# Two more pairs of split buffers ahead of the last gate: the tiles that brought m back are kept for it

## The chip, the cores and the metric

The kernel runs on one core of a Trainium2 chip. Five engines work beside each other: TensorE (PE in the profile, its weight loads PEld) multiplies, VectorE (DVE) and ScalarE (ACT) do elementwise work, GpSimd (POOL) some more of it, and SyncE (SP) issues most of the transfers. The metric is the device time of one execution in microseconds (us), lower is better. It is given as the median of several runs.

## The reference

One layer of a decoder trunk on 256 tokens of width 2048, all in float32:

```
h = rmsnorm(x);  u = h @ w_in                       # 16 half-width and 2 full-width fields
ya = b * conv3(c * xa) * silu(za)                   # branch A
yb = rmsnorm_per_head(hgrn2(q, f, iv)) * silu(og)   # branch B
m = sigmoid(ga) * (ya @ w_a) + sigmoid(gb) * (yb @ w_b)
x = x + m @ w_o
x = x + sigmoid(rmsnorm(x) @ w_pg) * (p @ w_pp)
out = rmsnorm(x)
```

The change touches the last two products, `m @ w_o` and `rmsnorm(x) @ w_pg`, both of a 256 x 2048 operand with a 2048 x 2048 weight.

## The kernel before

**Split products.** A float32 product is made from three reduced products. Each weight tile of 128 x 1024 that a load has brought (a half of a `raw` tile) is split by `cut` (lines 194 to 197): ScalarE copies it rounded into `whi`, VectorE subtracts and gets `wlo`. The operand is held split in the same way (`xh` and `xl`, or `mh` and `ml` for m), and `triple` issues hi x hi, hi x lo and lo x hi into one accumulator. So each weight tile costs one load of half a megabyte, one ScalarE and one VectorE instruction, and TensorE twelve matmuls of 512 columns (two token tiles, two slices of the contraction).

**Items and positions.** All weight tiles are laid in one list, `items`; the place in it is the position `pos` of the main loop. There are 275. Positions 213 to 244 are the four column groups of `m @ w_o` (kind O, eight tiles each, the first two interleaved). Positions 245 to 274 are the gate product (kind PG). Its first two column groups are computed together, at positions 245 to 258: for the chunks 3 and 5 of the contraction (`LATE_SEVEN`) by seven products of quarter blocks instead of eight (kind S, positions 251 and 254, 21 matmuls each), for the other six chunks plainly (kind C, two positions a chunk, 12 matmuls each). Group 2 is at 259 to 266, and the last, group 3, at 267 to 274 (`last_group`), which is run through three times, by token tile and half of the columns, so that its eight split pairs have to stay. The code calls position 245 `gate` and 254 `settled`.

**Buffers.** A split is put into a pair of buffers, which `free_pair` hands out. Four pairs lie in the pool `wp`. From position 245 on the pool `late`, opened in the place of the operand `m`, has five more; `rings` keeps per pool until which position each pair is taken, and the pool whose oldest pair comes free first gives it. Loads go to three `raw` tiles in `wp` (two positions each) and, for some chunks, to a fourth in `late`. `m` itself is written to DRAM for three of its four column groups and read back by `unpark` into tiles of the pool `back` (five tiles of 128 x 1024), transposed and split into `mT`. `back` is closed at position 229.

**How far ahead.** `ahead(pos)` says how many positions ahead of TensorE weights are split: 3, 4 from position 249, 5 from 255, growing to 8 at 265. Loads are issued four positions ahead of the splits, and wait for their `raw` tile.

**Chunks of seven products.** `combine_late` adds the quarter blocks of the raw tile of an S position on VectorE (four adds of 128 x 512), splits one quarter into a small pair `bhi` and `blo`, and at the next position splits the two rows of sums into two pairs (`free_pair`, twice). With the split that every position has, an S position takes three pairs.

**Epilogues.** They are generators that move on by one `yield` per position (`advance`; twice at an S position). `ep_o` adds a finished group of `m @ w_o` to x (line 879), squares it, writes it to DRAM and back to transpose it (`turned`: four writes, a read, after `lag` further steps the VectorE transpose of line 354), then splits it with a gain into `x1T` (lines 319 and 320). The lags are 3, 3, 6 and 7 for the four groups. `ep_products` (from line 752; the copy of line 756, the adds of line 747) puts the seven products together at position 256; it reads the PSUM banks P1, P6, P5 and P7. There are four banks of the kind "g"; group 2 of the gate takes the banks of P1 and P6 for its first and second token tile.

**What sets the order.** Instructions are emitted position by position: splits first, then matmuls, loads, epilogues. A planner orders each engine's instructions from that by its own estimate of when they are ready, TensorE's too. For ScalarE and VectorE `pinned` fixes the order of emission at positions 239 to 256 (and at 140 to 212). SP's and TensorE's queues stay the planner's. Each queue runs in order: what waits at its head holds what is behind it.

Of the kernel before, what the change touches and what calls it, by code (L numbers as in the profile page):

```python
# [9 lines left out]
F32 = mybir.dt.float32  # L10
F32R = mybir.dt.float32r
# [4 lines left out]
P = 128  # L16
# [7 lines left out]
CW = 512  # L24
# [24 lines left out]
def hybrid_kernel(ctx, tc, xT, x, pT, prm, gfin, masks, w_in, w_a, w_b, w_o, w_pg, w_pp, out):  # L49
    nc = tc.nc  # L50

    const = ctx.enter_context(tc.tile_pool(name="const", bufs=1))
    wp = ctx.enter_context(tc.tile_pool(name="wp", bufs=1))
# [6 lines left out]
    pools, closers = {}, {}  # L60

    def open_pool(name, side):
        closers[name] = ExitStack()
        pools[name] = closers[name].enter_context(
            tc.tile_pool(name=name, bufs=1, side=side, reuse_waits="tile")
        )

    def close_pool(name):
        closers.pop(name).close()
        del pools[name]  # L70
# [3 lines left out]
    state = {"tmp": "tmp1"}  # L74
# [3 lines left out]
    def nm(s):  # L78
        uid[0] += 1
        return f"{s}_{uid[0]}"  # L80

    def t4(tag="t4", bufs=None):
        bufs = bufs or {"tmp1": 8, "tmp2": 1, "tmp3": 5}[state["tmp"]]
        return pools[state["tmp"]].tile([P, 1024], F32, tag=tag, bufs=bufs, name=nm(tag))

    def bank(tag):
        return ps.tile([P, CW], F32, tag=tag, bufs=4, name=nm(tag))
# [19 lines left out]
    items = []  # L107
    for gi, (kind, j, w, g, op) in enumerate(groups):
# [3 lines left out]
        for c in range(w.shape[2]):  # L112
            it = {"gi": gi, "kind": kind, "j": j, "c": c, "last": c == w.shape[2] - 1, "op": op}
            if not units:
                key = ("PP", j // 2) if kind == "PP" else (gi, c // 2)
# [13 lines left out]
    def raw_of(pos):  # L129
        it = items[pos]  # L130
        if it["raw"] not in loaded:
            if it["kind"] == "S" and it["op"] == "hT":
                t = tuple(
                    pools["st"].tile([P, n, CW], F32, tag=tag, bufs=bufs, name=nm(tag))
                    for tag, n, bufs in (("sA", 2, 2), ("sB", 1, 3))
                )
            else:
                n = it["c"] if it["j"] == 0 else 4 + 4 * (it["j"] - 1) + it["c"] // 2
                spare = it["op"] == "x1T" and n and n % 4 == 0
                pool, bufs = (pools["late"], 1) if spare else (wp, 3)  # L140
                t = pool.tile([P, 2, 2 * CW], F32, tag="raw", bufs=bufs, name=nm("raw"))
            loaded[it["raw"]] = t
        return loaded[it["raw"]]
# [39 lines left out]
    def pair_of(pool, n, tags=("whi", "wlo"), width=2 * CW):  # L183
        return tuple(pool.tile([P, width], F32R, tag=tag, bufs=n, name=nm(tag)) for tag in tags)

    rings = {"wp": 4 * [-1], "late": 5 * [-1]}

    def free_pair(until):
        names = [n for n in rings if n == "wp" or n in pools]
        name = min(names, key=lambda n: rings[n][0])  # L190
        rings[name] = rings[name][1:] + [until if until < last_group else len(items)]
        return pair_of(pools.get(name, wp), len(rings[name]))

    def cut(hi, lo, src):
        a = nc.scalar.activation(out=hi, in_=src, func=AF.Copy)  # L195
        v = nc.vector.tensor_tensor(out=lo, in0=src, in1=hi.bitcast(F32), op=ALU.subtract)  # L196
        state["splits"] = (a.ins, v.ins)
# [15 lines left out]
    def combine_late(pos):  # L213
        R = raw_of(pos)
        (b11, b21), (b12, b22) = ([R[:, n, i * CW : (i + 1) * CW] for i in range(2)] for n in range(2))
        add(b11, b11, b12)
        add(b12, b12, b22)
        ts = [pair_of(pools["late"], 1, ("bhi", "blo"), CW)]
        cut(*ts[0], b22)
        add(b22, b11, b22)  # L220
        add(b21, b22, b21)
        yield
        for n in range(2):
            hi, lo = free_pair(pos)
            cut(hi, lo, R[:, n, :])
            ts += [(hi[:, i * CW : (i + 1) * CW], lo[:, i * CW : (i + 1) * CW]) for i in range(2)]
        b22, t1, t4_, t3, t2 = ts
        sums[pos] = (b22, t1, t3, t2, t4_)
# [15 lines left out]
    last_group = len(items) - w_pg.shape[2]  # L244
    gate = next(n for n, it in enumerate(items) if it["op"] == "x1T")
    settled = max(n for n, it in enumerate(items) if it["kind"] == "S")
# [3 lines left out]
    LEAD, AHEAD = 3, 4  # L250
    FIRST = 4
# [53 lines left out]
    def gain(base, k):  # L305
        return prm_t[:, base + k : base + k + 1]
# [28 lines left out]
    def blocks(ap):  # L335

        return ap.rearrange("p (c b e) -> p c b e", b=4, e=32)

    def spread(ap, t):

        return ap.rearrange("p (b c t e) -> p t c b e", b=4, c=4, t=NT)[:, t]

    def to_dram(src, tag, bufs, queue=nc.sync):
        d = dram.tile([P, 4, T], F32, tag=tag, bufs=bufs, name=nm(tag))
        to = d.rearrange("(b i) a x -> a i b x", b=4)
        for a in range(4):
            queue.dma_start(out=to[a], in_=src[32 * a : 32 * a + 32, :].rearrange("i (b x) -> i b x", b=4))  # L350
        return d

    def square_turn(dst, src):
        nc.vector.transpose(
            out=dst.rearrange("p (k a e) -> p a k e", a=4, e=32), in_=src.rearrange("p (a k e) -> p a k e", a=4, e=32)
        )

    def turned(src, lag, dst=None, queues=(nc.sync, nc.sync)):
        d = to_dram(src, "turn", 3, queues[0])
        yield  # L360
        queues[1].dma_start(out=src, in_=d.rearrange("p a x -> p (a x)"))
        for _ in range(lag):
            yield
        dst = t4() if dst is None else dst
        square_turn(dst, src)
        return dst
# [379 lines left out]
    def add(out, a, b):  # L746
        nc.vector.tensor_tensor(out=out, in0=a, in1=b, op=ALU.add)  # L747
# [100 lines left out]
            state["m", j] = to_dram(m, f"m{j}", 1)  # L848
            yield

    def back():
        return pools["back"].tile([P, 1024], F32, tag="back", bufs=5, name=nm("back"))

    def unpark():

# [18 lines left out]
    def ep_o(j, psum):  # L874
        xs = state["x"]
        src = t4()
        for t in range(NT):
            d = xs[:, t, j * CW : (j + 1) * CW]
            nc.vector.tensor_tensor(out=d, in0=d, in1=psum[t], op=ALU.add)
            nc.scalar.activation(  # L880
                out=src[:, t * CW : (t + 1) * CW], in_=d, func=AF.Square,
                accum_out=state["ss2"][:, t * 4 + j : t * 4 + j + 1],
            )
        x1 = src
        for t in range(NT):
            nc.scalar.activation(
                out=spread(x1, t), in_=blocks(xs[:, t, j * CW : (j + 1) * CW]), func=AF.Copy
            )
        x1 = yield from turned(x1, (3, 3, 6, 7)[j])
        for c in range(4):  # L890
            put(state["x1T"], j * 4 + c, x1[:, c * T : (c + 1) * T], gain(PRM_GPLE, j * 4 + c))
        for c in LATE_SEVEN:
            if c // 2 == j:
                yield
                yield from late_sums(c)
        if j == 3:
            tot = sc(2, "tot2", 1)
            nc.vector.tensor_reduce(
                out=tot, in_=state["ss2"].rearrange("p (t j) -> p t j", t=NT),
                axis=mybir.AxisListType.X, op=ALU.add,  # L900
            )
            state["rstd2"] = rsqrt_of(tot, NT, D, "r2")
# [212 lines left out]

    def ahead(pos):

        return LEAD + min(max(pos - gate, 0) // 4, 5 if pos > settled else 1)

    def triple(psum, op, part, first, last):  # L1120
        (oh, ol), (hi, lo) = op, part
# [7 lines left out]
    used, left = {}, {}  # L1129
# [57 lines left out]
    combining = {}  # L1187
    banks = {}
    psums = {}
    done = 0  # L1190
    for pos, it in enumerate(items[:last_group]):
        mark = len(nc.cur_bb.bb.instructions)
        kind, j, c, last = (it[n] for n in ("kind", "j", "c", "last"))
        _, _, w, g, opname = groups[it["gi"]]
        nch = w.shape[2]
        if kind == "O" and j == 2 and c == 0:
            close_pool("back")
        if pos == gate:
            close_pool("m")
            open_pool("late", "left")  # L1200
        if pos == parked:
            close_pool("st")
            open_pool("m", "left")
            state["mT"] = operand(pools["m"], "m", KT)
            open_pool("back", "left")
            active.append(unpark())
        if items[pos + 2]["kind"] == "S" and items[pos + 2]["op"] == "hT":
            combine_weights(pos + 2)
        for q in range(pos + 1, done):
            if items[q]["kind"] == "S" and items[q]["op"] != "hT" and q not in sums:  # L1210
                next(combining.setdefault(q, combine_late(q)), None)
        while done < min(pos + 1 + ahead(pos), len(items)):
            if done < 2:
                for i in range(2):
# [56 lines left out]
                for t in range(NT):  # L1271
                    product(psum[t], state[opname], k, t, hi[:, s], lo[:, s], k == 0, k == 2 * nch - 1)

        for q in range(done, min(done + AHEAD, len(items)) if pos >= FIRST else 0):
            load(q)
        if 0 <= pos - TOKENS < 4:
            load_tokens(pos - TOKENS)
# [33 lines left out]
    for t, halves in ((0, (0, 1)), (1, (0,)), (1, (1,))):  # L1311
        bk, n = bank("g"), CW // 2
# [16 lines left out]
    finish()  # L1329
    close_pool("tmp3")  # L1330
    close_pool("late")


# [70 lines left out]
```

## Time and profile before

| | |
|---|---|
| median of 3 runs | 816.7 us (816.34 to 816.7) |
| profiled execution | 815.29 us |
| its span in the profile | 813.5 us |
| TensorE busy | 802.3 us (99%) |
| VectorE busy | 607.0 us (75%) |
| ScalarE busy | 463.0 us (57%) |
| transfers | 198.52 MB, 244 GB/s on average |

Times in the profile count from the start of the span. A row of the timeline gives the start of an instruction, or of a run of like instructions (x and their number), its length, the engine, the line of the code, what it writes and reads, and in brackets how long the engine sat idle before it and what ended that. A wait for several things is put down to the one that came last. A matmul's length is a model, so a loss on TensorE is read from the distance between two starts. Windows give the busy time of each engine in a stretch of the span, with the number of instructions, the granted clock and the busy share of the DMA engines.

### The profile page before, as it was taken

To read this page: it belongs to the slowest core of one execution; us is meant where nothing else is said; L and a number is where in the kernel's file an instruction comes from. 1 tells how busy PE (TensorE), PEld (TensorE's weight loads), DVE (VectorE), ACT (ScalarE), POOL (GpSimd) and SP (SyncE) were. 2 spreads that over 40 slices of the span, in tenths; PEclk is the share of its full clock that TensorE was granted. 3 is DMA by queue.
4 is the path that set the end of the run, shared out by engine and by line. 5 is a ranking of instruction groups with operands and counts; after the bars stand their busy time and mean duration, and the time that the engine had idled before them with its cause. 6 is when DMAs were issued, how large, how long until landed. Compare 5 with 4: busy or idle time off the path is not lost.

```text
span 813.5 us, 10701 instructions
## 1 busy us (share of the span) xinstructions
PE 802.3 (99%) x4053; PEld 663.2 (82%) x4053; DVE 607.0 (75%) x780; ACT 463.0 (57%) x624; POOL 59.9 (7%) x58
## 2 busy tenths in 40 slices
PE   9999999999999999999999999999999999999995
PEld 6888888888888888888888888888888888887885
DVE  6746588767765498767679988987987656779972
ACT  7576476465555466466455556456545455665733
POOL 1000000001000000000021200210000000000280
PEclk9999999999999999999999999999999999999999
DMA  9988555648867555648799996996844779885722
GB/s 337 396 306 290 195 202 172 232 137 274 251 235 253 191 179 200 207 155 268 263 334 293 320 306 214 319 307 208 255 157 179 283 244 322 298 282 199 315 78 103
DMA packets 53812, 198.52 MB, mean 244 GB/s; under 512 B 6913, under 2 KB 16385, under 8 KB 40065
## 3 DMA queue, kind: packets, MB, share of 16 engines
q1 hardware_dynamic: 44352, 174.78, 60.7%
q0 software_dynamic: 6384, 16.25, 8.4%
q10 hardware_dynamic: 3024, 6.82, 2.5%
q8 instruction: 31, 0.51, 0.2%
q14 instruction: 21, 0.16, 0.1%
HBM read 184.19 MB, written 13.63 MB: 243 GB/s over the span
## 4 chain that ended last, share of the span: by engine, by line
PE 96%; issue 1%; ACT 1%; DMA 0%; DVE 0%; POOLq 0%; POOL 0%; ACTq 0%
PE g L1122 27%; PE g L1124 27%; PE g L1123 27%; PE s L1123 4%; PE s L1124 4%; PE s L1122 4%; PE s L530 1%; DMA praw<-in_pT 0%; ACT whi L195 0%; PE s L631 0%; PE s L650 0%; PE s L649 0%; PE s L648 0%; ACT xs L985 0%; ACT xh L319 0%
## 5 line engine op out<-in xcount | busy, mean ns | idle before, releaser
L196 DVE TENSOR_TENSOR wlo<-raw,whi 128x1024 fp32r<-128x1024 f32 (+1 forms) x266 | 319.0, 1216 | 151.4 <-ACT whi L195 149.6
L195 ACT ACTIVATE whi<-raw 128x1024 fp32r<-128x1024 f32 (+1 forms) x266 | 274.2, 1049 | 197.8 <-PE g L1124 163.9
L1122 PE MATMUL g<-whi,xh 128*128 128x512 f32 (+1 forms) x676 | 260.0, 385 | 0.0
L1124 PE MATMUL g<-whi,xl 128*128 128x512 f32 (+1 forms) x676 | 259.6, 384 | 0.0
L1123 PE MATMUL g<-wlo,xh 128*128 128x512 f32 (+1 forms) x676 | 259.6, 384 | 0.0
L1124 PEld LDWEIGHTS g<-whi,xl 128*128 128x128 f32 x676 | 127.0, 188 | 25.3
L1123 PEld LDWEIGHTS g<-wlo,xh 128*128 128x128 f32 x676 | 127.0, 188 | 25.0
L1122 PEld LDWEIGHTS g<-whi,xh 128*128 128x128 f32 x676 | 127.0, 188 | 24.8
L1123 PE MATMUL s<-wlo,xh 128*128 128x512 f32 x136 | 53.0, 390 | 0.0
L1124 PE MATMUL s<-whi,xl 128*128 128x512 f32 x136 | 53.0, 390 | 0.0
L1122 PE MATMUL s<-whi,xh 128*128 128x512 f32 x136 | 52.1, 390 | 0.2 <-ACT xh L319 0.2
L1123 PE MATMUL g<-wlo,mh 128*128 128x512 f32 x128 | 49.8, 389 | 0.0
L1124 PE MATMUL g<-whi,ml 128*128 128x512 f32 x128 | 49.7, 390 | 0.0
L1122 PE MATMUL g<-whi,mh 128*128 128x512 f32 x128 | 49.5, 389 | 0.0
L195 ACT ACTIVATE thi<-sA 128x1024 fp32r<-128x1024 f32 x15 | 15.9, 1062 | 32.4 <-DVE sA L747 20.1
L1122 PEld LDWEIGHTS s<-whi,xh 128*128 128x128 f32 x136 | 25.5, 188 | 5.8 <-ACT xh L319 0.6
L1123 PEld LDWEIGHTS s<-wlo,xh 128*128 128x128 f32 x136 | 25.5, 188 | 5.6 <-DVE wlo L196 0.3
L1124 PEld LDWEIGHTS s<-whi,xl 128*128 128x128 f32 x136 | 25.5, 188 | 5.5 <-DVE xl L320 0.2
L1124 PEld LDWEIGHTS g<-whi,ml 128*128 128x128 f32 x128 | 23.9, 188 | 5.2 <-DVE ml L830 0.3
L1122 PEld LDWEIGHTS g<-whi,mh 128*128 128x128 f32 x128 | 24.0, 188 | 5.0
L1123 PEld LDWEIGHTS g<-wlo,mh 128*128 128x128 f32 x128 | 24.0, 188 | 5.0
L1122 PE MATMUL g<-whi,yaTh 128*128 128x512 f32 x64 | 24.9, 389 | 0.0
(243 smaller groups left out, 980.8 us busy)
## 6 DMA issues: line engine op xcount, KB each, us to landing
raw<-in_w_in SPq DMA_DIRECT2D x66, 1024.0 KB, 4.9
raw<-in_w_o SPq DMA_DIRECT2D x16, 1024.0 KB, 6.3
sT<-in_w_in POOLq DMA_DIRECT2D x30, 512.0 KB, 9.6
raw<-in_w_in SPq DMA_DIRECT2D x28, 512.0 KB, 5.7
raw<-in_w_a SPq DMA_DIRECT2D x8, 1024.0 KB, 8.5
raw<-in_w_b SPq DMA_DIRECT2D x8, 1024.0 KB, 8.8
raw<-in_w_pg SPq DMA_DIRECT2D x16, 512.0 KB, 6.3
raw<-in_w_pg SPq DMA_DIRECT2D x8, 1024.0 KB, 7.2
```

The lines of the kernel that those rows point to most:

```text
L195: a = nc.scalar.activation(out=hi, in_=src, func=AF.Copy)
L196: v = nc.vector.tensor_tensor(out=lo, in0=src, in1=hi.bitcast(F32), op=ALU.subtract)
L530: nc.tensor.matmul(out, X[:, 0, h, s], X[:, 1, h, t], start=True, stop=True, tile_position=(0, i * n))
L1122: nc.tensor.matmul(psum, oh, hi, start=first, stop=False)
L1123: nc.tensor.matmul(psum, oh, lo, start=False, stop=False)
L1124: nc.tensor.matmul(psum, ol, hi, start=False, stop=last)
```

## The change

The tiles of `back` stay open to the end. At position 233 four of them are taken as two pairs of split buffers, and from there `free_pair` hands out, of all pairs in one list `held`, the one that comes free first: six pairs from 233, nine from 245 (three pairs in `late` in the place of five). `back` now lies below `m` on the stack, where `m` lay, and `late`, with three pairs and one raw tile, fills the place of `m`. The small pair `bhi`, `blo` becomes the two halves of a tile `t4` of the third part's pool.

`ahead` is 4 from position 233, 5 from 237 and 8 from 255. The loads run three positions ahead of the splits instead of four from 245 to 253. The fourth raw tile serves position 254 first instead of 252 (then 261 and 269). The second step of `combine_late` is taken two positions ahead of its S position at the earliest. The lag of the last group's transpose is 5 instead of 7.

```diff
-    def t4(tag="t4", bufs=None):
+    def t4(tag="t4", bufs=None, dtype=F32):
         bufs = bufs or {"tmp1": 8, "tmp2": 1, "tmp3": 5}[state["tmp"]]
-        return pools[state["tmp"]].tile([P, 1024], F32, tag=tag, bufs=bufs, name=nm(tag))
+        return pools[state["tmp"]].tile([P, 1024], dtype, tag=tag, bufs=bufs, name=nm(tag))
...
-                spare = it["op"] == "x1T" and n and n % 4 == 0
+                spare = it["op"] == "x1T" and n > 1 and n % 4 == 1
...
-    rings = {"wp": 4 * [-1], "late": 5 * [-1]}
+    held = []
 
     def free_pair(until):
-        names = [n for n in rings if n == "wp" or n in pools]
-        name = min(names, key=lambda n: rings[n][0])
-        rings[name] = rings[name][1:] + [until if until < last_group else len(items)]
-        return pair_of(pools.get(name, wp), len(rings[name]))
+        if "back" not in state:
+            held.append([until, pair_of(wp, 4)])
+            del held[:-4]
+            return held[-1][1]
+        it = min(held, key=lambda it: it[0])
+        assert it[0] < state["pos"]
+        it[0] = until if until < last_group else len(items)
+        return it[1]
...
-        ts = [pair_of(pools["late"], 1, ("bhi", "blo"), CW)]
+        b = t4(dtype=F32R)
+        ts = [(b[:, :CW], b[:, CW:])]
...
-    def back():
-        return pools["back"].tile([P, 1024], F32, tag="back", bufs=5, name=nm("back"))
+    def back(dtype=F32):
+        return pools["back"].tile([P, 1024], dtype, tag="back", bufs=5, name=nm("back"))
...
-        x1 = yield from turned(x1, (3, 3, 6, 7)[j])
+        x1 = yield from turned(x1, (3, 3, 6, 5)[j])
...
     def ahead(pos):
 
-        return LEAD + min(max(pos - gate, 0) // 4, 5 if pos > settled else 1)
+        if pos > settled:
+            return LEAD + 5
+        return LEAD + min(max(pos - gate + 16, 0) // 4, 2)
...
-        if kind == "O" and j == 2 and c == 0:
-            close_pool("back")
+        if pos == gate - 12:
+            state["back"] = [back(F32R) for _ in range(4)]
+            held.extend([-1, tuple(state["back"][i : i + 2])] for i in (0, 2))
         if pos == gate:
             close_pool("m")
             open_pool("late", "left")
+            held.extend([-1, pair_of(pools["late"], 3)] for _ in range(3))
         if pos == parked:
             close_pool("st")
+            open_pool("back", "left")
             open_pool("m", "left")
             state["mT"] = operand(pools["m"], "m", KT)
-            open_pool("back", "left")
             active.append(unpark())
...
             if items[q]["kind"] == "S" and items[q]["op"] != "hT" and q not in sums:
-                next(combining.setdefault(q, combine_late(q)), None)
+                if q not in combining or q <= pos + 2:
+                    next(combining.setdefault(q, combine_late(q)), None)
...
-        for q in range(done, min(done + AHEAD, len(items)) if pos >= FIRST else 0):
+        for q in range(done, min(done + AHEAD - (gate <= pos < settled), len(items)) if pos >= FIRST else 0):
             load(q)
...
     close_pool("late")
+    close_pool("back")
```

More of the change, by code (lines that the diff above doesn't have):

```diff
@@ L1191, in hybrid_kernel @@
     for pos, it in enumerate(items[:last_group]):
-        mark = len(nc.cur_bb.bb.instructions)
+        mark, state["pos"] = len(nc.cur_bb.bb.instructions), pos
         kind, j, c, last = (it[n] for n in ("kind", "j", "c", "last"))
```

## The prediction

> **What bounds the kernel now.** I read the page first, for the engine that fills the span and the chain that ended last.
>
> ```profile
> span 813.5 us, 10701 instructions
> ## 1 busy us (share of the span) xinstructions
> PE 802.3 (99%) x4053; PEld 663.2 (82%) x4053; DVE 607.0 (75%) x780; ACT 463.0 (57%) x624; POOL 59.9 (7%) x58
> ```
>
> TensorE is the bound. The change takes no matmul away, so it can win only what TensorE loses in idle time. The view of what TensorE waited for and the windows of the last stages say how much that is and where.
>
> ```profile
> PE s L1014 <- DVE warm L1010: 1.5, 1, 1.5
> PE g L1122 <- ACT whi L195: 0.7, 2, 0.4
> PE s L1122 <- ACT xh L319: 0.2, 1, 0.2
> ```
>
> ```profile
> 629.00:716.30 87.30, 87.30 (x385) 72.02 (x385) 58.52 (x65) 47.22 (x65) 0.57 (x1) 1.00 0.82 290
> 716.30:744.80 28.50, 28.50 (x126) 23.38 (x125) 24.79 (x33) 15.13 (x22) 0.00 (x0) 1.00 0.80 280
> 744.80:749.10 4.30, 3.44 (x13) 1.78 (x12) 3.50 (x9) 4.26 (x7) 0.72 (x1) 1.00 0.00 2
> 749.10:760.40 11.30, 11.30 (x51) 9.36 (x50) 11.02 (x12) 8.52 (x10) 0.00 (x0) 1.00 0.84 323
> ```
>
> The first wait is at the start of the kernel and stays. The other two fall into one window of 4.3 us. Before and after it TensorE is full: 126 matmuls in 28.50 us, 0.226 us each. TensorE's timeline there (four rows of one matmul each left out) tells the loss exactly.
>
> ```profile
> 744.82 0.39 PE L1124 MATMUL s<-whi,xl 128*128 128x512 f32 x1
> 745.40 0.50 PE L1122 MATMUL s<-whi,xh 128*128 128x512 f32 x1 [0.20 <-ACT xh L319]
> ...
> 746.72 0.39 PE L1124 MATMUL s<-whi,xl 128*128 128x512 f32 x1
> 747.55 0.50 PE L1122 MATMUL g<-whi,shi 128*128 128x512 f32 x1 [0.44 <-ACT whi L195]
> 747.88 0.40 PE L1122 MATMUL s<-whi,xh 128*128 128x512 f32 x1
> 748.50 0.73 PE L1122 MATMUL g<-whi,shi 128*128 128x512 f32 x2 [0.22 <-ACT whi L195]
> 749.07 0.39 PE L1123 MATMUL g<-wlo,shi 128*128 128x512 f32 x1
> ```
>
> From 744.82 to 749.07 are 4.25 us, in which 11 matmuls started: 4.25 - 11 x 0.227 = 1.75 us lost. TensorE first waits for the last group's `xh`, the tail of `m @ w_o`, and then for the two combined pairs of position 254. This 1.75 us, 0.21% of 816.7, is all that the change can win. VectorE's and ScalarE's timelines say who made TensorE wait.
>
> ```profile
> 719.44 1.28 DVE L879 TENSOR_TENSOR xs<-xs,g 128x512 f32<-128x512 f32 x2
> 723.66 1.23 DVE L196 TENSOR_TENSOR wlo<-raw,whi 128x1024 fp32r<-128x1024 f32 x1 [2.94 <-ACT whi L195]
> ...
> 725.74 1.22 DVE L196 TENSOR_TENSOR wlo<-raw,whi 128x1024 fp32r<-128x1024 f32 x1
> ...
> 727.47 2.35 DVE L196 TENSOR_TENSOR wlo<-raw,whi 128x1024 fp32r<-128x1024 f32 x2
> 729.86 1.42 DVE L747 TENSOR_TENSOR raw<-raw 128x512 f32<-128x512 f32 x2
> ...
> 733.25 5.76 DVE L196 TENSOR_TENSOR wlo<-raw,whi 128x1024 fp32r<-128x1024 f32 x5
> ...
> 742.43 1.22 DVE L196 TENSOR_TENSOR wlo<-raw,whi 128x1024 fp32r<-128x1024 f32 x1
> 743.57 1.24 DVE L354 STREAM_TRANSPOSE t<-t 128x1024 f32<-128x1024 f32 x1
> ```
>
> ```profile
> 744.84 1.71 ACT L319 ACTIVATE xh<-t,prm_t 128x256 fp32r<-128x256 f32 x4 [6.99 <-DVE t L354]
> 746.46 6.73 ACT L195 ACTIVATE whi<-raw 128x1024 fp32r<-128x1024 f32 x7
> 754.75 1.06 ACT L195 ACTIVATE whi<-raw 128x1024 fp32r<-128x1024 f32 x1 [1.56 <-DMA raw<-in_w_pg]
> 755.71 0.58 ACT L756 ACTIVATE t<-g 128x512 f32<-128x512 f32 x1
> ```
>
> From 723.66 VectorE works without a pause up to the transpose at 743.57; ScalarE stands 6.99 us in front of `xh`, behind that transpose. VectorE's queue in the order of emission is the limit of this stage, not the transfer of the transpose.
>
> **The change part by part.**
>
> *Split buffers and the lead.* Pairs free from position 233 let two splits more be done before the gate. After the add to x at 719.44, VectorE has ten splits ahead of the transpose now (the rows of 1, 1, 2, 5 and 1). With two positions more of lead these begin at position 250 in place of 248, and with lag 5 the transpose still stands behind the split of 255: eight splits. Two splits are 2.35 us (the row at 727.47). So the transpose comes at 743.57 - 2.35 = 741.22 and `xh` at 742.49, ahead of the 744.82 at which TensorE wants it. Its wait goes.
>
> The two splits move to 684 to 716, where in the window from 629 VectorE is busy 58.52 of 87.30 us, ScalarE 47.22. Their loads (a megabyte) go there too; DMA engines are free for 18% of those 87.3 us, 15.7 us. I cost them at nothing: TensorE has three split positions in hand, 36 matmuls, 8.2 us. If that cover went, it would cost TensorE the wait for a load. One place there is tight: group 2's transpose already waits for its DMA, and the add at 719.44 is behind it in the queue.
>
> ```profile
> 713.73 1.25 DVE L354 STREAM_TRANSPOSE t<-t 128x1024 f32<-128x1024 f32 x1 [0.33 <-DMA t<-turn]
> ```
>
> Each microsecond by which an early split holds up group 2's write would come off the 2.35. Bounds: 0, and 1.2 for one split; I take 0, since `back` is free before TensorE gives a pair back, which lets a split start earlier.
>
> *What is late next: the combined pairs of 254.* They now stand behind the split of 256. VectorE takes up its splits 3.96 us after the transpose:
>
> ```profile
> 747.53 8.04 DVE L196 TENSOR_TENSOR wlo<-raw,whi 128x1024 fp32r<-128x1024 f32 x7 [0.19 <-ACT whi L195]
> 755.84 1.23 DVE L196 TENSOR_TENSOR wlo<-raw,whi 128x1024 fp32r<-128x1024 f32 x1 [0.28 <-ACT whi L195]
> 756.98 0.68 DVE L747 TENSOR_TENSOR t<-t,g 128x512 f32<-128x512 f32 x1
> ```
>
> That is 741.22 + 3.96 = 745.18 now, and 1.15 us for each of seven: 256, the two of 254, then 257 to 260. The second of 254 is ready at 745.18 + 3 x 1.15 = 748.6, 1.2 earlier than now (749.83). TensorE can meanwhile run position 255, 12 matmuls or 2.7 us from 745.05, to 747.8, and then the first pair's six, 1.4 us, to 749.1. No wait if the planner orders it so; up to 0.5 us if it takes 254's four first matmuls as early as now. The next bound covers that.
>
> *The new queue in front of the banks.* At position 255 the lead jumps to 8: four splits (260 to 263), and 264 at 256, are emitted ahead of `ep_products`, and the order is pinned there. Before, only 261 stood between 260 and `ep_products` (the single rows at 754.75 and 755.84). Position 259, group 2, needs the banks that `ep_products` reads: its second token tile wants P6, free with the add at 756.98, while it starts only here:
>
> ```profile
> 760.42 0.39 PE L1122 MATMUL g<-whi,xh 128*128 128x512 f32 x1
> ```
>
> With 1.75 us won it starts at 758.67 and wants P6 three matmuls on, at 759.35. When is P6 free? The load of 261 waits for its raw tile, released by the second split of 254, as now:
>
> ```profile
> 749.91 22.82 SPq L160 DMA_DIRECT2D raw<-in_w_pg  x7
> DMA to landing us min/median/max: 4.7/7.2/7.9
> ```
>
> (The second line gives the landing times of all the gate's megabyte loads.) It is issued 0.08 us after that split, 748.7. From issue to ScalarE's start took 754.75 - 749.91 = 4.84 us: 753.5. VectorE follows 1.09 later (755.84 against 754.75), 754.6; four splits, 4.6; the add, 0.68: 759.9. Against 759.35 that is a delay of 0.57. Bounds by the fastest and slowest landing of the gate's megabyte loads, 4.7 and 7.9 us: delay 0.4 and 3.6. I take 4.84, the same load from the same releaser, at a time when the DMA engines stand idle (share 0.00 in the window up to 749.1). The load of 263, issued 2.3 us ahead, is the only other one.
>
> [...] No run here shows this load in its new place; the 4.84 above is the nearer row.
>
> *What costs nothing.* The `t4` tile in place of `bhi`, `blo`: the same two instructions each, and the slots it takes were last used by group 1's sums and group 2's transpose, long done; cover gone, the adds of 254 wait behind it. The exchange of `back` and `m` in memory: SP's reads of m might wait for other tiles than now, with the loads of `w_o` queued behind; bounds 0 and the stage's lead of 8.2 us, taken as 0. The new places of the raw tile and one load less of lead: 254 takes the room of `m`, free at 716.3, 19 us ahead of its split. The other queues, POOL and the scalar DMA queue, get nothing new. The last group is split at the pace of freed pairs as now, and TensorE does not wait there.
>
> Sum: -1.75 + 0.57 = -1.18, and 0.08 for handing over, as from split to load above: -1.1 us. The profiled execution is 815.29, which gives 814.2; the median is 1.4 above it, so 816.7 - 1.1 = 815.6.
>
> **The rivals.**
>
> *All of it is won.* The planner knows the banks and can give TensorE the first token tile's matmuls of 259 and 260, 12 of them, 2.7 us, before it wants P6. For it speaks that TensorE's order now mixes products (`s` rows between `g` rows above); against it, that a fine order rests on the planner's guess of the load. Time: 816.7 - 1.75 = 814.95, and with a little scatter on either side.
>
> *Slower: five splits before the banks.* The load of 261 lands late, or ScalarE waits in its pinned queue for 263's. Gain and loss are equal where P6 comes 1.75 after 759.35, that is with a landing of 6.0 us; from 7.7 us it is slower by over 0.2%. At 7.9 the sum is -1.75 + 3.6 = +1.9: 818.6. For it speaks the median of 7.2; against it that this median has several loads in flight.
>
> *No head start.* The two splits are not done by the gate, because loads of `w_o` land as late as now or group 2 is held up. The transpose is at 743.57 again, 254's second pair behind 256 at 751.0, the load of 261 at 751.1, P6 at 762.3 against 761.1 for TensorE without the gain: +1.2, 817.9.
>
> **How the numbers follow.** About 0.2%, 1.6 us, is what a measurement of this kernel can tell from no change. Forecast (815.6, its own range 815.1 to 816.5): 0.43. All won: 0.27. Slower by the banks: 0.21. No head start: 0.09. Faster by over 0.2% is the second, and a hair of the first: 0.28; slower by over 0.2% the third and a little of the fourth: 0.23; within it the rest, 0.49. The range must reach to both of the large rivals: 814.7 to 818.4.
>
> **What would show it.** VectorE's last transpose near 741.2, not 743.6, and eight splits between the add to x and it; no wait of TensorE for `xh`; the two waits for `whi` at 747 to 749 gone or under 0.5 us. ScalarE's copy of P1 (line 756) near 758 instead of 755.7, behind five `whi`, the first of which waits for its load; a wait of TensorE for VectorE at the start of group 2 near 759. The forecast is wrong if that wait is over 2 us, if TensorE waits for a load at 684 to 716, or if the transpose has not moved.

## The result, and the profile after

The changed kernel takes 814.3 us in the median (813.43 to 816.03). The kernel before, run beside it on the same chip, takes 816.13 us (815.19 to 816.9). The ratio is 0.998, with a 95% interval of 0.9972 to 0.9989: 1.8 us faster, by the interval 0.9 to 2.3. 814.3 lies 0.4 us below the range of the prediction and 1.3 below its time. Of the 1.3, 0.57 is the starting point (816.13 against the 816.7 from which the sum was taken); the rest is the change, -1.83 in place of -1.1, and -1.1 lies inside that interval.

The profiled execution of the changed kernel is not a typical one. It took 816.03 us, the longest of its kernel, and was longer than the profiled execution of before (815.29). So its trace shows the mechanism, but not the median. Its span is 814.3 us. First the view of what TensorE waited for behind 640 us (us in total, times, longest).

```profile
PE g L1129 <- ACT t L761: 1.2, 1, 1.2
PE g L1129 <- ACT whi L199: 0.2, 1, 0.2
```

The wait for `xh` is gone, of the two waits for `whi` one of 0.2 is left, and a new one has come: TensorE waits for `t` of line 761, the copy of P1 in `ep_products` (line 756 before). The windows and TensorE's timeline show where.

```profile
744.50:749.30 4.80, 4.55 (x19) 3.13 (x18) 4.49 (x9) 4.80 (x8) 0.72 (x1) 1.00 0.16 24
749.30:759.40 10.10, 10.10 (x46) 8.35 (x45) 7.18 (x7) 5.90 (x7) 0.00 (x0) 1.00 0.95 373
759.40:761.50 2.10, 0.85 (x4) 0.42 (x3) 2.10 (x3) 2.10 (x4) 0.00 (x0) 1.00 0.69 222
```

```profile
747.71 0.50 PE L1129 MATMUL g<-whi,shi 128*128 128x512 f32 x1 [0.22 <-ACT whi L199]
...
759.40 0.39 PE L1131 MATMUL s<-whi,xl 128*128 128x512 f32 x1
761.04 0.50 PE L1129 MATMUL g<-whi,xh 128*128 128x512 f32 x1 [1.25 <-ACT t L761]
761.37 0.39 PE L1130 MATMUL g<-wlo,xh 128*128 128x512 f32 x1
```

From 759.40 to 761.37 two matmuls started in 1.97 us: 1.97 - 2 x 0.227 = 1.52 us lost at the start of group 2. Around 747 about 0.8 us is still lost (18 matmuls from 744.52 to 749.43). Together 2.3, against 1.75 for the same stretch of before. VectorE's timeline and then ScalarE's tell why.

```profile
715.31 1.25 DVE L359 STREAM_TRANSPOSE t<-t 128x1024 f32<-128x1024 f32 x1
...
742.76 1.24 DVE L359 STREAM_TRANSPOSE t<-t 128x1024 f32<-128x1024 f32 x1
...
757.69 3.50 DVE L200 TENSOR_TENSOR wlo<-raw,whi 128x1024 fp32r<-128x1024 f32 x3 [2.92 <-ACT whi L199]
761.11 1.22 DVE L200 TENSOR_TENSOR back<-raw,back 128x1024 fp32r<-128x1024 f32 x1
762.24 0.68 DVE L752 TENSOR_TENSOR t<-t,g 128x512 f32<-128x512 f32 x1
```

```profile
702.36 1.06 ACT L199 ACTIVATE back<-raw 128x1024 fp32r<-128x1024 f32 x1 [2.28 <-DMA raw<-in_w_o]
...
712.84 1.06 ACT L199 ACTIVATE back<-raw 128x1024 fp32r<-128x1024 f32 x1 [3.09 <-DMA raw<-in_w_pg]
...
756.60 2.96 ACT L199 ACTIVATE whi<-raw 128x1024 fp32r<-128x1024 f32 x3 [4.20 <-DMA raw<-in_w_pg]
759.46 1.04 ACT L199 ACTIVATE back<-raw 128x1024 fp32r<-128x1024 f32 x1
760.41 0.58 ACT L761 ACTIVATE t<-g 128x512 f32<-128x512 f32 x1
```

Three things are to be seen. The last transpose came 0.81 us earlier than before (742.76 against 743.57), not 2.35, because all of this stage moved later with group 2's transpose (715.31 against 713.73). Before `ep_products` ScalarE stood 4.20 us in front of a load, and then did four splits before the copy of P1 at 760.41. The DMA view has that load (transfers issued from 748.8 to 750.9: engine, operation, number, KB, us from issue to landing), and SyncE's timeline has its issue.

```profile
raw<-in_w_pg SPq DMA_DIRECT2D x1, 1024.0 KB, 6.2
```

```profile
750.26 0.33 SPq L160 DMA_DIRECT2D raw<-in_w_pg  x1
```

### The profile page after: what moved, and what is told of

Same layout as the page of the kernel before. It is cut to its first block, busy times and chain, and to the rows that moved or that the text cites. A ratio compares the mean times of both kernels' runs of the same rounds, so it can differ in the third digit from the quotient of the medians.

```text
span 814.3 us, 10705 instructions
## 1 busy us (share of the span) xinstructions
PE 802.5 (99%) x4053; PEld 663.7 (82%) x4053; DVE 607.3 (75%) x780; ACT 463.6 (57%) x624; POOL 59.0 (7%) x58
## 4 chain that ended last, share of the span: by engine, by line
PE 87%; DMA 4%; DVE 3%; ACT 2%; issue 2%; SPq 1%; ACTq 0%; POOLq 0%; POOL 0%; DVEq 0%
PE g L1129 25%; PE g L1130 25%; PE g L1131 25%; PE s L1130 3%; PE s L1131 3%; PE s L1129 3%; DMA raw<-in_w_o 2%; DMA turn<-t 1%; DVE wlo L200 1%; DMA raw<-in_w_pg 1%; SPq L355 1%; DMA t<-turn 1%; ACT back L199 1%; PE s L535 1%; DVE back L200 0%
## 5 line engine op out<-in xcount | busy, mean ns | idle before, releaser
L200 DVE TENSOR_TENSOR wlo<-raw,whi 128x1024 fp32r<-128x1024 f32 (+1 forms) x254 | 304.1, 1214 | 145.6 <-ACT whi L199 143.7
L199 ACT ACTIVATE whi<-raw 128x1024 fp32r<-128x1024 f32 (+1 forms) x254 | 261.9, 1050 | 190.3 <-PE g L1131 164.8
L1129 PE MATMUL g<-whi,xh 128*128 128x512 f32 (+1 forms) x656 | 253.2, 386 | 1.2 <-ACT t L761 1.2
L1131 PE MATMUL g<-whi,xl 128*128 128x512 f32 (+1 forms) x656 | 252.7, 385 | 0.0
L1130 PE MATMUL g<-wlo,xh 128*128 128x512 f32 (+1 forms) x656 | 252.7, 385 | 0.0
L1130 PE MATMUL s<-wlo,xh 128*128 128x512 f32 x120 | 46.7, 389 | 0.0
L1131 PE MATMUL s<-whi,xl 128*128 128x512 f32 x120 | 46.7, 389 | 0.0
L1130 PE MATMUL g<-wlo,ybTh 128*128 128x512 f32 x64 | 24.9, 389 | 0.0
L1131 PE MATMUL g<-whi,ybTl 128*128 128x512 f32 x64 | 24.9, 389 | 0.0
L1130 PE MATMUL g<-wlo,yaTh 128*128 128x512 f32 x64 | 24.9, 389 | 0.0
```

Of the source, the lines that this page charges most:

```text
L1129: nc.tensor.matmul(psum, oh, hi, start=first, stop=False)
L1130: nc.tensor.matmul(psum, oh, lo, start=False, stop=False)
L1131: nc.tensor.matmul(psum, ol, hi, start=False, stop=last)
```

## The experiments

All kernels below compute the whole layer. Each ratio is against the kernel before in runs beside it. "Lost" is TensorE's loss behind 640 us, from the distances of its starts less 0.227 us for each matmul, as above. Line numbers in the rows of this kernel and its variants are 4 to 7 higher than those of before (matmuls 1129 to 1131 for 1122 to 1124, `cut` 199 for 195).

**The same kernel again.** No edit.

> The changed kernel once more, for a second profiled execution. In the first one ScalarE waited 2.28 us at 702.36 and 3.09 us at 712.84 for loads, which held up group 2's turn and left only 0.8 us of the head start of 2.35, and ScalarE waited 4.20 us for the load of 261. Theory 1 (the head start is real, and late loads take it back in some executions): this execution differs in those three waits, and its span follows them: with all three under 1 us the last transpose lies near 741.2 and TensorE loses under 0.5 us between 740 and 762. Theory 2 (the waits are part of the order of work): the same three waits come again, within 0.5 us, and the gain of the median is from somewhere else. Time 814.3, ratio 0.997 to 0.999.

815.77 against 815.65 us, ratio 1.0000 (0.999 to 1.0009). The gain of the first comparison is not there. The profiled execution (815.48, span 813.7) lost 2.2 us, nearly all of it at the start of group 2. TensorE's timeline:

```profile
758.36 0.39 PE L1131 MATMUL s<-whi,xl 128*128 128x512 f32 x1
760.47 0.50 PE L1129 MATMUL g<-whi,xh 128*128 128x512 f32 x1 [1.72 <-ACT t L761]
760.80 0.40 PE L1130 MATMUL g<-wlo,xh 128*128 128x512 f32 x1
```

2.44 us less two matmuls is 1.99. At 745 to 749 nothing was lost: its transpose stood at 741.70, `xh` came in time. ScalarE's waits for loads at 701 and 712 us were shorter than in the first profile (1.15 and 1.40 us in place of 2.28 and 3.09, with one of 2.21 at 709 that the first did not have), and the one ahead of `ep_products` was longer (4.69 in place of 4.20). So in this execution the change does win the old loss and puts one of about the same size in its place, 13 us later.

**Only the lag.** The kernel before with the lag of 5 and nothing else.

```diff
-        x1 = yield from turned(x1, (3, 3, 6, 7)[j])
+        x1 = yield from turned(x1, (3, 3, 6, 5)[j])
```

> The kernel before with the last group's lag at 5 and nothing else. Rival (the lag alone is the change): the transpose and xh come earlier, TensorE's waits at 745 to 749 go, 814.3 to 814.7. Theory 1 (the two splits done before the gate are what counts): the transpose moves ahead of the adds of 254 and the split of 255, 4.6 us, to about 739, but these come as much later, so that TensorE waits for 255 or for 254's pairs in place of xh: 815.5 to 817, no gain over 0.1%.

815.64 against 815.65, ratio 1.0003 (0.9994 to 1.0011). An earlier transpose alone brings nothing; here a wait for splits takes the place of the wait for `xh`. Its profiled execution was its longest (818.45). VectorE's transposes and TensorE's waits:

```profile
716.55 1.25 DVE L354 STREAM_TRANSPOSE t<-t 128x1024 f32<-128x1024 f32 x1 [3.22 <-DMA t<-turn]
...
741.76 1.24 DVE L354 STREAM_TRANSPOSE t<-t 128x1024 f32<-128x1024 f32 x1
```

```profile
726.51 0.73 PE L1122 MATMUL s<-whi,xh 128*128 128x512 f32 x2 [1.94 <-ACT whi L195]
727.77 0.50 PE L1123 MATMUL s<-wlo,xh 128*128 128x512 f32 x1 [0.52 <-DVE wlo L196]
...
750.05 0.50 PE L1122 MATMUL g<-whi,shi 128*128 128x512 f32 x1 [1.81 <-ACT whi L195]
```

The read of group 2's turn landed 2.8 us later than in the profile of before (716.55 against 713.73), and the splits queued behind that transpose came late for TensorE at 726.5. From 724.19 to 728.11 four matmuls started, 3.0 us lost. The lag of the last group acts only behind this place, so this wait exists without the change too, in executions in which that read is late; the execution from which I took the 1.75 lost 0.1 us there.

**The jump two positions later.** With the lead at 5 until 256, only the split of 261 stands ahead of `ep_products`, as before the change.

```diff
-        if pos > settled:
+        if pos > settled + 2:
             return LEAD + 5
```

> The changed kernel, with the jump of the lead to 8 two positions later, so that one split and not five stands between 260 and the putting together of the seven products. Theory 1: TensorE's wait for the bank of P1 (1.5 us lost in the first profile of the changed kernel) goes, the copy of P1 comes behind a single load; 0.3 to 1.5 us faster than the changed kernel, 812.8 to 814.0. Rival (that wait was one execution's late load): no difference from the changed kernel, within 0.3 us of it.

813.91 (813.09 to 814.22) against 815.65, ratio 0.9976 (0.9966 to 0.9986). On the same chip the change itself gave 1.0000. Windows over the same stretches, then VectorE's transposes and ScalarE's rows:

```profile
744.50:749.30 4.80, 4.80 (x23) 3.98 (x22) 4.80 (x5) 4.80 (x6) 0.62 (x1) 1.00 0.53 162
...
759.40:761.50 2.10, 2.10 (x11) 1.75 (x10) 2.10 (x4) 1.40 (x2) 0.00 (x0) 1.00 0.93 300
```

```profile
713.08 1.24 DVE L359 STREAM_TRANSPOSE t<-t 128x1024 f32<-128x1024 f32 x1
...
740.53 1.24 DVE L359 STREAM_TRANSPOSE t<-t 128x1024 f32<-128x1024 f32 x1
```

```profile
754.36 1.06 ACT L199 ACTIVATE whi<-raw 128x1024 fp32r<-128x1024 f32 x1 [1.48 <-DMA raw<-in_w_pg]
755.33 0.58 ACT L761 ACTIVATE t<-g 128x512 f32<-128x512 f32 x1
```

The load of 261 took as long as in the changed kernel (6.3 us from its issue at 748.03 to 754.36), but one split stands between it and the copy of P1, not four, and TensorE finds the bank free. (While it waited for that load, ScalarE did two splits of another one that had landed earlier, at 750.86 and 751.83.) In this execution (span 811.3, the fastest of seven) TensorE lost 0.2 us behind 640. So with the new queue ahead of the banks the new wait goes too; a second profile of this kernel, below, does not have it either.

**Without the early splits.** The lead of before up to position 254, with everything else of the change.

```diff
-        return LEAD + min(max(pos - gate + 16, 0) // 4, 2)
+        return LEAD + min(max(pos - gate, 0) // 4, 1)
```

> The changed kernel without the two earlier splits: its lead grows as before up to 254, so the two pairs from back are there and nothing is split earlier. Theory 1: VectorE has ten splits again in this stage, the gain goes, 815.7 to 816.8. Rival (the pairs, the raw tile or the lag make the gain): 814.3, as the changed kernel.

817.44 against 815.65, ratio 1.0026 (1.0014 to 1.0037). Slower than before, and slower than I expected: what remains of the change costs 1.8 us, and the early splits win that back. In the profiled execution the last transpose came early (738.55), since fewer splits stand ahead of it, and TensorE waited for the first pair of 254, which is split behind it:

```profile
745.00 0.39 PE L1131 MATMUL s<-t,slo 128*128 128x512 f32 x1
746.93 0.50 PE L1129 MATMUL g<-whi,shi 128*128 128x512 f32 x1 [1.53 <-ACT whi L199]
```

That execution was the fastest of its kernel (815.54). It lost 2.1 us behind 640, hardly more than the first profile of before on the same count (2.0), so it does not show where the median of 817.44 comes from.

**The same kernel a third time**, on another chip, where all that follows was run.

> The changed kernel a third time, so that the next three have it on their chip. Its ratio to the kernel before was 0.998 the first time and 1.000 the second. Theory 1 (the wins at 745 and the loss at the start of group 2 hang on when loads land, here 6.2 and 6.7 us after issue for that of 261): a ratio between 0.997 and 1.001, and a profile in which TensorE's loss at the start of group 2 is what the landing of 261 makes of it: copy of P1 at the landing plus 3.8 us. Rival (the second time was a bad chip): 0.998 again.

815.1 (813.9 to 817.93) against 815.86, ratio 0.9994 (0.9983 to 1.0005). The profiled execution (816.99) lost 3.6 us, 1.75 of it at group 2, where ScalarE copied P1 only at 761.38. All three profiled executions of the changed kernel have that wait, and in all three the copy of P1 came 3.9 us behind the landing of the load of 261 (3.8 expected): landings at 756.49, 755.92 and 757.47, copies at 760.41, 759.84 and 761.38. ScalarE took up its splits 0.1 us behind each landing. The executions of the first comparison between 813.43 and 814 us (span 811.7 to 812.2) seem to have no room for it: the shortest profile of all, that of the late jump, has a span of 811.3, lost 0.2 behind 640, and lost less ahead of 640 than any other profile. None of them has a profile of its own.

**A second late raw tile.** The other way to take the load out of the queue: let it start earlier. The room comes from the fifth tile of `back`.

```diff
-                pool, bufs = (pools["late"], 1) if spare else (wp, 3)
+                pool, bufs = (pools["late"], 2) if spare else (wp, 3)
...
-        return pools["back"].tile([P, 1024], dtype, tag="back", bufs=5, name=nm("back"))
+        return pools["back"].tile([P, 1024], dtype, tag="back", bufs=4, name=nm("back"))
```

> The changed kernel with a second raw tile in late (and four tiles in back in the place of five), so that the load of 261 does not wait for the pairs of 254 and goes out some 12 us earlier; all five splits still stand before the seven products. Theory 1 (the late load of 261 makes the wait at the start of group 2): the copy of P1 comes at 755 to 757 in place of 760, TensorE's wait there goes, 1 to 2 us faster than the changed kernel beside it. Rival (the five splits as such, five of 1.0 us on ScalarE, or the kept pairs): the wait stays, within 0.4 us of the changed kernel.

814.33 (813.53 to 815.33) against 815.86, ratio 0.9979 (0.997 to 0.9987). ScalarE did its splits ahead of `ep_products` without a wait and copied P1 4.5 us earlier than in the changed kernel. TensorE has no wait at group 2. Against the changed kernel on the same chip the median is 0.8 us lower, a little less than the 1 to 2 us expected.

```profile
755.95 0.57 ACT L761 ACTIVATE t<-g 128x512 f32<-128x512 f32 x1
```

So to remove the wait either half is enough: fewer splits behind the load, or an earlier load.

**The late jump with the old lag, and without the early splits.** Two variants of the late jump that undo one part of the change each.

```diff
-        x1 = yield from turned(x1, (3, 3, 6, 5)[j])
+        x1 = yield from turned(x1, (3, 3, 6, 7)[j])
```

> The changed kernel with the later jump and the lag of the last group at 7 again. Theory 1 (the head start of two splits is what brings xh in time; the lag only lets the transpose pass one split): the transpose comes at most 1.2 us later, xh still before 744.8, within 0.5 us of the changed kernel with the later jump: 813.5 to 814.4. Rival (the lag is needed): 1 us or more slower than that, 814.9 to 815.5.

```diff
-        return LEAD + min(max(pos - gate + 16, 0) // 4, 2)
+        return LEAD + min(max(pos - gate, 0) // 4, 1)
```

> The changed kernel with the later jump and without the two earlier splits. Theory 1: the gain of 1.75 us goes with the head start: 815.3 to 816.5, as the kernel before. Rival (the jump was the only thing that mattered, and the rest is worth nothing or the whole gain without the early splits): 813.7 to 814.3, as with the later jump alone.

With lag 7: 814.33 against 815.86, ratio 0.9984 (0.9976 to 0.9993). The wait for `xh` came back with half a microsecond (0.8 us by the distance of the starts), no more:

```profile
PE s L1129 <- ACT xh L324: 0.5, 1, 0.5
```

Without the early splits: 817.46, ratio 1.0023 (1.0013 to 1.0033), above the 815.3 to 816.5 that I expected; the profiled execution (815.13) was again the fastest and does not show why. So the early splits, which the added pairs make possible, are the part that carries the gain; that of the lag is too small to be told here.

**Before and the late jump once more.** The kernel before, one execution, and the late jump with no further edit.

> The kernel before once more, for a second profiled execution; its first had 1.75 us of loss at 744 to 749, and its span of 813.5 lies low among its times. Theory (group 2's turn lands late in many executions; without splits in hand that reaches TensorE): VectorE waits over 0.5 us for that turn at 713, and TensorE loses over 1.5 us after 640, at 744 to 749 or, as in the execution of the lag alone, 2.9 us at 726. Rival (the first execution is the common one): the same 1.6 to 1.9 us at 744 to 749 and nothing at 726.

> The changed kernel with the later jump again, on whatever chip this is. Theory 1: 0.997 to 0.9985 of the kernel before, 813.2 to 814.5, and a loss of TensorE after 640 under 1 us. Rival (0.9976 was that chip): 0.999 to 1.000.

The execution of before (816.99, span 815.2) lost 2.3 us behind 640: 1.7 at 746 to 750, for the reasons shown in the prediction and as much as in the first profile, and 0.45 at a late split at 726; the other 0.2, at 662, is in every profile. So both my theory and its rival were half right. Of the 1.7 us by which its span is longer than the first, 1.4 had arisen before 663. Its two transposes stand 29.85 us apart, as in the first profile.

```profile
715.44 1.25 DVE L354 STREAM_TRANSPOSE t<-t 128x1024 f32<-128x1024 f32 x1 [0.66 <-DMA t<-turn]
745.29 1.24 DVE L354 STREAM_TRANSPOSE t<-t 128x1024 f32<-128x1024 f32 x1
```

The late jump gave 814.82 (813.23 to 817.88) against 815.69, ratio 0.9989 (0.9976 to 1.0001), less than at first. Its profiled execution (816.14) lost about 0.8 us at 748 to 749, group 2's transpose having waited 1.35 us for its read, and more at the start of the kernel, where the change has no part:

```profile
717.01 1.25 DVE L359 STREAM_TRANSPOSE t<-t 128x1024 f32<-128x1024 f32 x1 [1.35 <-DMA t<-turn]
```

```profile
12.53 0.50 PE L1130 MATMUL s<-wlo,pop 128*128 128x512 f32 x1 [0.77 <-DVE wlo L200]
```

The wait at group 2 stayed away.

**A later head start.** If the early splits' loads delay group 2's turn, splits that begin four positions later should leave it alone.

```diff
-        return LEAD + min(max(pos - gate + 16, 0) // 4, 2)
+        return LEAD + min(max(pos - gate + 12, 0) // 4, 2)
```

> The later jump, and the two earlier splits begun at positions 237 and 241 in place of 233 and 237, so that they do not stand before the squares of group 2 on ScalarE, where waits of 0.6 to 2.3 us for w_o loads held up its turn. Theory 1 (these waits eat the head start in some executions): as fast as the later jump or up to 0.5 us faster, with a narrower spread. Rival (the later begin has too few splits done by the gate): 0.5 to 1.5 us slower than the later jump.

A miss: 816.44 against 815.69, ratio 1.0006 (0.9994 to 1.0017). VectorE's rows:

```profile
716.43 1.23 DVE L200 TENSOR_TENSOR wlo<-raw,whi 128x1024 fp32r<-128x1024 f32 x1 [4.02 <-ACT whi L199]
...
718.84 1.24 DVE L359 STREAM_TRANSPOSE t<-t 128x1024 f32<-128x1024 f32 x1
```

```profile
715.33 1.06 ACT L199 ACTIVATE whi<-raw 128x1024 fp32r<-128x1024 f32 x1 [4.18 <-DMA raw<-in_w_pg]
```

Group 2's transpose did not wait for its read. It stood in the order of emission behind two splits (the second, left out above, from 717.70), and ScalarE (the last row) waited 4.18 us for the first one's load. So what held group 2 up in this execution was the splits queued ahead of its transpose, and with them the load for which the first of these stood 4.18 us, not its own read.

**Both cures.** The late jump and the second raw tile together.

> The later jump and the second raw tile in late together. Theory 1 (what is left after the later jump is the late turn of group 2, from loads at 700 to 717, which neither touches): as the later jump, 0.9975 to 0.999 of the kernel before, 813.5 to 814.9; a loss of TensorE at the start of group 2 of nothing. Rival (late loads after 746 still cost executions that were not profiled): better than the later jump, below 0.9975.

A second miss, and a plain one: 817.45 (816.63 to 818.12) against 815.38, ratio 1.0024 (1.0014 to 1.0034). VectorE's transpose, ScalarE's rows, then windows around TensorE's loss (after the commas the busy times of PE, PEld, DVE, ACT and POOL, then the granted clock):

```profile
743.54 1.24 DVE L359 STREAM_TRANSPOSE t<-t 128x1024 f32<-128x1024 f32 x1
```

```profile
745.62 1.06 ACT L199 ACTIVATE whi<-raw 128x1024 fp32r<-128x1024 f32 x1 [7.80 <-PE s L1131]
746.59 1.69 ACT L324 ACTIVATE xh<-t,prm_t 128x256 fp32r<-128x256 f32 x4
```

```profile
745.00:748.90 3.90, 1.83 (x7) 0.93 (x6) 2.19 (x4) 3.27 (x6) 0.00 (x0) 1.00 0.00 0
748.90:752.30 3.40, 3.40 (x9) 2.64 (x9) 3.37 (x7) 3.40 (x5) 1.63 (x1) 0.50 0.22 34
```

The transpose ended at 744.8, but `xh` began at 746.59. ScalarE had a split ahead of it that waited 7.80 us for a pair from TensorE. The order of ScalarE's instructions in the two kernels shows that it is position 262's, which is emitted behind the pinned stretch; with its load earlier the planner was free to put it ahead of `xh`, and did. What TensorE then lost in this execution was not only the wait (below).

## Why the prediction was wrong

Two steps of the sum failed: the time it starts from, by which the forecast left the measured time outside its range, and the charge for the banks, by which its mechanism was off.

*The start, 816.7.* The prediction subtracted from the median of three executions. Beside the changed kernel the median of thirteen was 816.13, and in the later runs those of 31 and 35 were 815.65 and 815.86. With 816.13 the forecast would have been 815.0 and the lower end of the range 814.1, below the measured 814.3. The other 0.7 us of the miss is the change itself, -1.83 for -1.1. One comparison cannot tell these apart, and the two repeats gave 0.1 and -0.8.

*The ceiling, 1.75 us.* The prediction said that this "is all that the change can win". No run shows that to be wrong for a median: the first comparison won 1.83, the late jump 1.74 and 0.87. But 1.75 is the loss of one execution, 1.4 us faster than the median from which I subtracted it. The other execution of before lost 1.7 at the same place and 0.45 at 726. One with the lag alone, the longest of its kernel, lost 3.0 at 726, where the early splits are two ahead and the trace of the changed kernel has no wait. So the head start may also be a reserve against late reads; that is argued, not shown.

*Two splits, 2.35 us.* Right. Counted from group 2's transpose, to which the queue is tied, the last one came after 29.84 and 29.85 us before and after 27.45 us in the changed kernel (742.76 - 715.31, the same in the two other profiles) and in the late jump (740.53 - 713.08): 2.39 less.

*The early splits at nothing.* Open. My bounds were 0 and 1.2 us. Group 2's transpose came 0.5 to 2.3 us later than in the profile I read, at 715.31, 714.25 and 716.06 in the three profiles of the changed kernel, against 713.73. In the first the rows of ScalarE at 702.36 and 712.84 show how: splits that wait for loads stand ahead of group 2's work in the pinned order. But the late jump has the same early splits, and there it came at 713.08. In all eight profiles with them it lies between 713.08 and 717.01, in the five without between 713.17 and 716.55. These overlap, and part of the spread had arisen before this stage, so the shift is not shown to be the change's.

*The combined pairs of 254.* About right: the prediction allowed 0 to 0.5 us. The second profile lost nothing there, the first 0.2 by the view of waits and 0.8 by the distances.

*Five splits before the banks, +0.57 us.* This step failed: the queue was right, the bank and the size were not. The prediction priced P6, on which TensorE would wait for VectorE. In all three profiles TensorE waited for P1, behind ScalarE's copy, and that cost 1.5, 2.0 and 1.75 us. I expected the load to be issued at 748.7 and P6 free at 759.9; in the profile it was issued at 750.26 and P6 was free at 762.24 + 0.68 = 762.92. Of the 3.0 us between, 1.5 is the late transpose (742.76 against 741.22), and 1.5 the load: ScalarE started 6.34 us behind the issue, not 4.84. A megabyte load was in flight ahead of it and one behind it, where the row of before had nothing ahead of it. From issue to landing this load took 6.2 us, the loads before and behind it 4.9 and 6.4. TensorE did not pay the whole 3.6 us (762.92 - 759.35) but 1.5 to 2.0, since the planner had the first token tile's bank, P1's, taken first: there half of the first rival ("all of it is won") was right, too.

*No head start.* This rival gave +1.2 us. Without the early splits it was +1.8 (817.44 against 815.65) and, with the late jump, +1.6. The sign is right, the place is not, as far as the profiles show it: the transpose was early, and the pairs of 254 were late.

*What stays open.* The change measured 0.998, 1.0000 and 0.9994. In the three profiles 0.8, 0 and 1.6 us of the old loss remained, and the new wait of 1.5 to 2.0 came on top. That explains a kernel that is even with the one before, or slower. It does not explain the 1.8 us of the first comparison, which no profile shows. If its faster executions did without the new wait, as their spans suggest, the step that failed there is that the wait is not in every execution. The wait hangs on the landing of one load and on group 2's read, and in the three profiles the landing differs by 1.55 us (755.92 to 757.47) and group 2's transpose by 1.81 (714.25 to 716.06); that this made the difference is argued, not shown.

## What to carry to other kernels

A loss read from one profiled execution is that execution's, and a median of three is not yet the kernel's: set both against the spread of more runs before a gain of 0.2% is added up from them. When a change gives an in-order queue more to do ahead of a release (here splits ahead of the copy that frees a bank), price the slowest thing that each of these instructions waits for with the transfers that will then be in flight, not with the quietest row of the trace (here 6.34 us from issue to the split, where that row had 4.84); the cheap cure is to put the extra work behind the release, and here that gave 0.9976 and 0.9989 where the change itself gave 0.998 to 1.0000 (the two are told apart on one chip only, 0.9976 against 1.0000). Two cures that each remove the same wait need not add up, since a planner reacts to each of them.

## What the runs showed of the hardware

In one profile a stall of TensorE cost more than its length. In the kernel with both cures TensorE stood 1.70 us, ran two matmuls, and stood 0.69 us. Then the granted clock was 0.50 from about 748.9 to 752.3, and matmuls started 0.43 us apart in place of 0.227. Its timeline:

```profile
745.20 0.39 PE L1131 MATMUL s<-whi,xl 128*128 128x512 f32 x1
747.13 0.50 PE L1129 MATMUL s<-back,xh 128*128 128x512 f32 x1 [1.54 <-ACT xh L324]
747.47 0.39 PE L1130 MATMUL s<-back,xh 128*128 128x512 f32 x1
748.39 0.50 PE L1131 MATMUL s<-back,xl 128*128 128x512 f32 x1 [0.52 <-DVE xl L325]
...
749.00 0.63 PE L1130 MATMUL s<-back,xh 128*128 128x512 f32 x1
749.43 0.63 PE L1131 MATMUL s<-back,xl 128*128 128x512 f32 x1
```

These 3.4 us cost another 1.6 us: eight matmuls started in them, and at 0.227 us apart it would have been fifteen. The lengths of the stops do not decide it alone. The kernel with the lag alone stood 2.10 us, ran two matmuls and stood 0.69 (the rows at 726.51 and 727.77 above), and its clock stayed at 1.00 in the windows from 725 to 729. At the end of the kernel, where TensorE has run out of work, the clock went to 0.50 as well: in the profile of before at 810.0, 5.4 us behind the last matmul (804.57, that matmul counted as 0.12 us, the distance of the starts there), in the first profile of the changed kernel at 808.1, 2.8 us behind it (805.33). What decides when the clock falls is not shown.

The mean granted clock of a whole execution was 0.996 to 0.998 in all executions of the kernels before and after, but 0.994 in nine executions of the two kernels without early splits (817.5 to 820.1 us). 3.4 us at clock 0.50 take 0.002 off the mean of a span of 816, so these may have lost the clock as well; that is an estimate, they have no profile. In the kernel with both cures two of nine executions have 0.994; the other seven (816.63 to 818.07) are slow without it.

Three megabyte loads in a row, about 2.3 us apart, took longer from the first to the last. In the DMA view of the changed kernel, for the stretches 747.5 to 748.8, 748.8 to 750.9 and 750.9 to 753:

```profile
raw<-in_w_pg SPq DMA_DIRECT2D x1, 1024.0 KB, 4.9
```

```profile
raw<-in_w_pg SPq DMA_DIRECT2D x1, 1024.0 KB, 6.4
```

The first had nothing ahead of it and took 4.9 us, the second is the load of 261 with its 6.2, the third took 6.4. In the other two profiles of this kernel, too, a later load took longer than the one ahead of it: 6.7 and 6.9 us for the load of 261 and the next one in the second, 4.9 and 6.5 for the one ahead and that of 261 in the third.
